# Cosine attention on one core: V cast two pairs at once, twelve sums of squares moved to TensorE, other ring sizes and new instruction orders

## The chip, the core and the metric

The kernel runs on one core of a Trainium2 chip. A core has five engines that work side by side: PE (TensorE, matmuls), ACT (ScalarE, functions such as the exponential), DVE (VectorE), POOL (GpSimd) and SP (SyncE, which here only issues DMAs). Each executes its own list of instructions strictly in order, and they wait for each other through semaphores. The metric is the device time of one execution in microseconds, lower is better. Before the change three runs took 189.35, 189.43 and 189.87 us: the median is 189.43 us.

## What is computed

```python
batch, heads, seq, dim = 8, 12, 512, 64          # float32 inputs, tau = 0.1
Q_norm = Q / (np.linalg.norm(Q, axis=-1, keepdims=True) + 1e-10)
K_norm = K / (np.linalg.norm(K, axis=-1, keepdims=True) + 1e-10)
scores = np.einsum('bhqd,bhkd->bhqk', Q_norm, K_norm) / tau
weights = np.exp(scores - np.max(scores, axis=-1, keepdims=True))
weights = weights / (np.sum(weights, axis=-1, keepdims=True) + 1e-10)
return np.einsum('bhqk,bhkd->bhqd', weights, V).astype(np.float32)
```

Scores of normalized vectors lie between -10 and 10, so the kernel takes no maximum off before the exponential.

## The kernel before

The 96 heads are worked on as 48 pairs of heads, numbered s = 0 to 47. For each pair:

- SP loads Q and K (256 KB each, `LD`, L311) and V (`LV`, L314), and stores the result (`ST`, L565).
- POOL squares Q and K of the pair in one instruction of 128x1024 (`SQ`, L337). The squares are summed over the 64 dimensions. For K this is done by PE in most pairs (`SSQ`, L354: eight small matmuls against the identity that fold 64 columns to 8, into columns 320 to 383 of one of the two accumulator banks of the values) followed by a small reduction on DVE (`RED`, L361). For Q from pair 4 on it is a reduction of 128x512 on DVE (`RED`, L365).
- For a group of one, two or four pairs DVE computes 1/norm by a few small instructions (`NEW`, L389 to L398).
- Q is scaled on DVE, K mostly on POOL (`SCL`, L420), into the ring `qn`. PE transposes both (`TR`, L426) into one PSUM bank, DVE copies that to SBUF (`EVA`, L434).
- The scores are made in four chunks of 128 keys (`SCO`, L508: two matmuls, one for each head, with 64 rows and 512 columns). Two chunks fit in PSUM. ACT takes the exponential of each chunk, 128x1024 (`EXP`, L531). A score chunk can start when the exponential of the chunk two before it is done.
- In pairs 37 and 45 chunk 3 is not done on ACT: its exponential is a polynomial on DVE and POOL (`SCX`, `X`, `Y`, L473 to L486).
- POOL casts V to bf16 (`VC`, L536) into `vb`, which carries a column of ones beside each block of 64 columns. PE multiplies the exponentials with it (`PV`, L548: eight groups of four matmuls, each group one block of 128 queries of one head, summed over the four chunks). Each head has its own accumulator bank.
- DVE takes the reciprocal of the sums (`RCP`, L559) and multiplies (`NRM`, L561) into the ring `ob`.

The next pair's values of the same head can start in a bank only after this pair's `NRM`, and, where an `SSQ` was placed in that bank behind the pair's values, after its `RED` too (`session`, `attached`, `bank_free`).

The program first lists all operations with what each needs. `ORDER` then gives, written out by hand as numbers, the order in which each engine executes them. Nothing is rescheduled at run time. The sizes of the rings stand in one line: `RINGS = 15, 10, 6, 4, 4, 4, 8, 3` for Q/K loads with cast V, V loads, squares, scaled Q and K, transposed Q and K, exponentials, output, and norms. An operation that fills a slot needs the last reader of what was in it, so for instance `LD` of pair s needs `SCL` and `SQ` of pair s - 15, and `NRM` of pair s needs `ST` of pair s - 8.

Of the kernel before, what the change touches and what calls it, by code (L numbers as in the profile page):

```python
# [5 lines left out]
ALU = mybir.AluOpType  # L6
# [13 lines left out]
class Program:  # L20
# [5 lines left out]
    def add(self, key, eng, kind, due, needs, emit, **kw):  # L26
        assert key not in self.ops, key
        op = Op(key, eng, kind, due, needs, emit, **kw)
        self.ops[key] = op
        self.list.append(op)  # L30
        return op

# [76 lines left out]
def bass_cosine_similarity_attention_kernel(  # L109
# [20 lines left out]
    qk = [sb(f"qk{i}", [128, 2, 2, NT * DIM], f32) for i in range(R_QK)]  # L130
    vf = [sb(f"vf{i}", [128, 2, NT * DIM], f32) for i in range(R_V)]
    vb = sb("vb", [128, R_QK, NT, 2, DIM + 1], bf16)
    sq = [sb(f"sq{i}", [128, 16, DIM], bf16) for i in range(R_SQ)]
    qn = [sb(f"qn{i}", [128, 2, NT, 2, DIM], bf16) for i in range(R_QN)]
# [16 lines left out]
    o_ps = [nc.alloc_psum_tensor(f"ops{b}", [128, 512], f32) for b in range(2)]  # L151
# [25 lines left out]
    def key(name, s, *rest):  # L177
# [9 lines left out]
        vb[:, :, :, :, DIM : DIM + 1].rearrange("p r c h o -> p (r c h o)"), 1.0))  # L187
# [14 lines left out]
    def due_red(s):  # L202
        return due_sq(s) + 2.0
# [9 lines left out]
    for s, w in sorted(((s, w) for s in range(NP) for w in range(2) if on_pe(s, w)), key=lambda j: (due_red(j[0]), j)):  # L213
        at = due_red(s) + 0.3
        if s < EARLY:
            early.append((s, w))
            continue
        due, i, h = next(x for x in slots if x[0] >= at and (x[1], x[2]) not in attached)
        attached[i, h] = (s, w)
        session[s, w] = (h, due, [("PV", i, h, NT - 1)])  # L220
# [5 lines left out]
    for s in range(NP):  # L226
        for h in range(2):
            bank_free[s, h] = before[h]
            before[h] = [("NRM", s, h)] + ([("RED",) + attached[s, h]] if (s, h) in attached else [])
# [67 lines left out]
    def pair(s):  # L297
# [6 lines left out]
        for w, x in ((0, Q), (1, K)):  # L304
            if s == 0:
# [8 lines left out]
              lambda e: e.dma_start(out=vf[iv][:, :, :], in_=src(V, s)), slot=f"v{iv}")  # L314
# [99 lines left out]
        for w in range(2):  # L414
# [3 lines left out]
            P.add(("SCL", s, w), "dve" if dve else "pool", "sclq" if dve else "sclk", T0 - (2.85 if w and not dve else 2.55) - slack(s, M_SCL),  # L418
                  [("NEW", g, (7 if direct_r(g) else 6) if acts and dve else 6 + w + (dve and w))] + ([("UNIT", s)] if s in off_of and w == 0 else []) + ([("TR", 0, w, 0), ("TR", 0, w, 1)] if s == R_QN else [key("TR", s - R_QN, w)]),
                  lambda e, w=w, r=r: e.tensor_tensor(  # L420
                      out=qn[iqn][:, w].rearrange("p t h d -> p h t d"),
                      in0=qk[iq][:, w].rearrange("p h (t d) -> p h t d", t=NT), in1=r, op=ALU.mult))
# [71 lines left out]
    def rest(s):  # L494
# [3 lines left out]
        for c in range(NT):  # L498
# [26 lines left out]
            for hs in ((0,), (1,)) if s == 0 and c < 2 else ((0, 1),):  # L525
# [9 lines left out]
        P.add(("VC", s), "pool", "vc", T0 + 3.0 - slack(s, M_VC), [("LV", s), key("PV", s - R_QK, 0, NT - 1), key("PV", s - R_QK, 1, NT - 1), "vone"],  # L535
              lambda e: e.tensor_scalar(  # L536
                  out=vb[:, iq, :, :, 0:DIM].rearrange("p c h d -> p h c d"),
                  in0=vf[iv][:, :, :].rearrange("p h (c d) -> p h c d", c=NT),
                  scalar1=1.0, scalar2=1.0, op0=ALU.mult, op1=ALU.mult))
# [3 lines left out]
        for h in range(2):  # L543
            for i in range(NT):
                def pv(e, h=h, i=i):
                    for c in range(NT):
                        t = i
                        last = e.matmul(  # L548
                            out=o_ps[h][:, 65 * t : 65 * t + 65],
                            lhsT=et[iet][:, c, h, 128 * t : 128 * t + 128], rhs=vb[:, iq, c, h, :],  # L550
                            start=(c == 0), stop=(c == NT - 1))
                    return last

                need, due = sum((exps(s, c) for c in range(NT)), []), T0 + PERIOD + 0.9 * PV_AT[4 * h + i] + late(s)
                P.add(("PV", s, h, i), "pe", "pv", due, need + [("VC", s)] + (bank_free[s, h] if i == 0 else [("PV", s, h, i - 1)]), pv)
            grid = o_ps[h][:, 0 : 65 * NT].rearrange("p (t x) -> p t x", x=65)
# [6 lines left out]
                      in1=rd[io][:, h, :].unsqueeze(2).to_broadcast([128, NT, DIM]), op=ALU.mult))  # L563
        P.add(("ST", s), "sp", "ld", s + STORE_AT, [("NRM", s, i) for i in range(2)],
              lambda e: e.dma_start(out=src(out, s), in_=ob[io][:, :].rearrange("p h t d -> p h (t d)")), slot=f"out{io}")  # L565

    def last(s, T0):
        iq, iet, io = s % R_QK, s % R_ET, s % R_O
        spare = t_ps[:, :, :, :].rearrange("p w t x -> p (w t x)").bitcast(f32)
        for k, (h, lo, hi) in enumerate(PIECES):  # L570
            bank = spare if k == 2 else o_ps[h]
            for c in range(NT):
                def pv(e, h=h, lo=lo, hi=hi, c=c, bank=bank):
                    for t in range(lo, hi):
# [3 lines left out]
                            rhs=vb[:, iq, c, h, :], start=(c == 0 and t == lo), stop=(c == NT - 1), skip_group_check=True)  # L578
# [29 lines left out]
OFF = {(45, 3): ((45, 45), False), (37, 3): ((37, 37), False)}  # L608
# [7 lines left out]
PE_BOTH = 4  # L616
BY_VECTOR = (35, 39, 43, 47)
Q_ON_PE = ()
# [3 lines left out]
RINGS = 15, 10, 6, 4, 4, 4, 8, 3  # L622
# [17 lines left out]
def slack(s, most):  # L640
# [5 lines left out]
        "7 8 64 65 103 104 11 141 142 66 179 180 105 222 223 143 256 257 181 298 299 224 332 333 258 375 376 300 "  # L646
        "409 410 334 451 452 63 377 102 411 140 453 178 221 485 486 527 528 561 562 487 604 605 529 638 639 255 "
        "563 680 681 297 606 714 715 331 640 756 757 374 682 790 791 408 716 833 834 450 758 867 868 484 792 901 "
        "902 526 835 935 936 560 869 978 979 603 903 1012 1013 637 937 1046 1047 679 980 1080 1081 713 1014 1122 "
        "1123 1048 1156 1157 1082 1190 1191 755 1124 1224 1225 789 1158 1267 1268 832 1192 1301 1302 866 1226 "  # L650
        "1335 1336 900 1269 1368 1369 934 1303 1411 1412 977 1337 1456 1457 1011 1370 1490 1491 1045 1413 1523 "
        "1524 1079 1458 1566 1567 1121 1492 1600 1601 1155 1525 1634 1635 1189 1568 1667 1668 1223 1602 1709 1710 "
        "1266 1636 1754 1755 1300 1669 1788 1789 1334 1711 1756 1790 1367 1410 1455 1489 1522 1565 1599 1633 1666 "
        "1708 1753 1787 1816 1830 "
    ),
    "pool": (
        "2 0 1 4 14 27 22 35 69 107 50 144 145 89 182 225 127 165 259 208 301 231 335 378 273 284 307 242 454 412 "
        "437 350 395 471 361 318 488 530 426 460 564 607 641 502 536 683 513 717 579 547 759 590 793 836 655 689 "
        "870 624 666 904 742 731 765 700 938 981 808 819 776 876 1015 1049 910 1083 853 887 921 1125 1066 953 "
        "1159 987 964 1021 1108 998 1193 1032 1304 1227 1338 1097 1270 1131 1165 1414 1371 1142 1199 1493 1242 "  # L660
        "1176 1310 1459 1569 1210 1343 1603 1253 1526 1287 1386 1321 1397 1354 1421 1637 1670 1465 1712 1436 1437 "
        "1438 1439 1476 1442 1509 1575 1552 1791 1586 1757 1609 1642 1740 1620 1684 1719 1653 1763 1774 1809 1695 "
        "1796 1734 1735 1736 1737 "
# [4 lines left out]
        "264 139 265 233 266 132 267 133 268 338 269 270 176 271 170 379 171 305 275 177 213 336 214 219 381 220 "  # L668
        "339 340 309 341 342 455 343 253 344 345 346 348 247 415 248 413 347 352 382 254 289 457 384 416 290 417 "
        "386 295 418 296 419 489 420 323 421 491 423 324 329 422 330 424 458 428 531 366 533 367 492 372 493 565 "  # L670
        "494 373 495 462 496 608 497 400 567 401 499 498 406 500 407 642 504 534 610 442 568 443 569 448 570 449 "
        "571 684 572 538 573 476 575 574 644 577 477 611 718 581 482 576 483 613 686 518 645 519 646 760 647 615 "
        "648 524 649 525 650 552 720 652 651 553 653 837 794 558 657 796 559 595 762 687 721 596 722 871 723 691 "
        "724 601 725 839 726 602 728 629 873 727 630 729 635 905 636 733 763 907 671 797 798 672 799 677 800 801 "
        "678 802 767 804 803 939 806 705 941 706 840 711 805 712 810 982 908 842 747 984 748 753 754 844 874 1050 "
        "781 1018 782 787 788 878 1016 1084 1052 824 942 825 943 944 912 945 830 946 831 947 949 948 950 951 858 "
        "1086 859 864 865 985 955 1019 1160 898 899 892 1128 893 1126 989 1055 1053 932 1162 933 926 927 1023 975 "
        "1194 976 1196 1087 969 1088 970 1089 1090 1305 1091 1057 1092 1228 1093 1094 1003 1095 1009 1004 1230 "
        "1010 1129 1339 1099 1340 1271 1043 1037 1273 1038 1044 1163 1133 1307 1197 1071 1231 1415 1232 1077 1072 "
        "1233 1078 1234 1372 1235 1167 1236 1119 1113 1238 1237 1120 1114 1240 1201 1308 1495 1274 1153 1239 1341 "  # L680
        "1374 1154 1147 1276 1148 1460 1244 1187 1494 1181 1417 1182 1570 1278 1462 1188 1375 1215 1376 1216 1377 "
        "1312 1378 1221 1379 1222 1380 1604 1382 1381 1345 1418 1384 1264 1419 1258 1265 1259 1383 1388 1463 1498 "
        "1527 1423 1292 1529 1298 1293 1431 1299 1432 1326 1572 1639 1434 1327 1435 1496 1638 1606 1713 1530 1332 "
# [86 lines left out]
```

## Time and profile before

| | us |
|---|---|
| median of three runs | 189.43 |
| the profiled execution | 189.84 |
| its span, first to last instruction | 187.9 |
| ACT busy | 180.8 |
| PE busy | 173.7 |
| DVE busy | 172.3 |
| POOL busy | 166.8 |

The page counts an engine as busy while it executes; waiting and issuing are not counted. Matmuls are pipelined, so PE's busy time is not its work. A group's row gives line, engine, operation, tiles out and in, shape and count, then busy time, the mean duration of one in ns, and the idle time before them with what ended it. The duration of one instruction can be longer than the distance from its start to the next one's start, as neighbours overlap. The chain that ended last is followed back from the last instruction; in order of time its rows are start, length and what ran. A timeline row is start, length, engine, line, operation and count.

Activity by stage (busy us and instructions of each engine, then granted clock, DMA share and GB/s), from the view of stretches:

```
15.00:60.00 45.00, 43.18 (x692) 27.31 (x688) 44.25 (x156) 45.00 (x52) 43.80 (x37) 1.00 1.04 344
60.00:96.00 36.00, 34.95 (x572) 22.58 (x568) 34.49 (x119) 36.00 (x41) 35.46 (x31) 1.00 0.96 311
96.00:140.00 44.00, 41.58 (x673) 26.48 (x673) 43.28 (x132) 44.00 (x49) 43.87 (x38) 1.00 0.96 320
140.00:176.00 36.00, 33.14 (x506) 20.14 (x505) 33.84 (x98) 35.99 (x40) 32.15 (x30) 1.00 0.38 121
176.00:187.90 11.90, 7.79 (x137) 5.04 (x136) 7.30 (x21) 8.46 (x11) 0.82 (x1) 1.00 0.34 112
```

The columns of engines are PE, PEld (weight loads), DVE, ACT and POOL.

### The profile page before, as it was taken

Reading aid. Unit: us, or ns where it says so; the run is one execution under the profiler, and the core shown is the slowest. Engines: PE = TensorE matmul, PEld = TensorE weight load, DVE = VectorE, ACT = ScalarE, POOL = GpSimd, SP = SyncE. Lnnn points to the kernel's source line nnn. Section 1 sums busy time; section 2 is a strip of 40 time slices with the busy share of each in tenths; the row PEclk is TensorE's granted clock in tenths of the full one; section 3 lists DMA queues with packets and bytes.
Section 4 is the critical chain, followed back from the end, with each engine's and each line's share of the span. In section 5 each row is a group of like instructions: output and inputs, shape, how many; then the busy total and the mean of one; then the engine's idle time right before and its main releaser. Section 6 shows DMA issues by size and latency. Waiting matters only on the chain.

```text
span 187.9 us, 6635 instructions
## 1 busy us (share of the span) xinstructions
PE 173.7 (92%) x2694; PEld 108.7 (58%) x2694; DVE 172.3 (92%) x546; ACT 180.8 (96%) x212; POOL 166.8 (89%) x152
## 2 busy tenths in 40 slices
PE   6999999999998999999999999899999989999983
PEld 2655666566665666666666556556645446655552
DVE  2789999999999999999999999999999999988864
ACT  4799999999999999999999999999999999999992
POOL 4797999999999999999999999999999999696600
PEclk9999999999999999999999999999999999999999
DMA  4999999899999988999999999976996551312215
GB/s 148 356 350 349 348 354 331 233 328 370 379 385 375 326 243 264 333 304 297 361 379 381 380 380 301 306 244 198 302 336 194 173 167 59 112 59 76 95 59 169
DMA packets 52446, 50.76 MB, mean 270 GB/s; under 512 B 3136, under 2 KB 52416, under 8 KB 52416
## 3 DMA queue, kind: packets, MB, share of 16 engines
q1 hardware_dynamic: 51984, 50.02, 81.1%
q8 instruction: 21, 0.34, 0.8%
q10 hardware_dynamic: 432, 0.33, 0.5%
q14 instruction: 9, 0.07, 0.1%
HBM read 37.75 MB, written 12.58 MB: 268 GB/s over the span
## 4 chain that ended last, share of the span: by engine, by line
ACT 92%; PE 4%; DMA 1%; DVE 1%; issue 1%; POOL 0%
ACT et L531 90%; DMA qk<-in_Q_dram 1%; PE ops L548 1%; PE scps L508 1%; DVE xs L245 0%; PE ops L576 0%; ACT ys L379 0%; DVE ob L589 0%; PE scps L268 0%; POOL qn L258 0%; ACT nps L382 0%; PE tps L268 0%; ACT sq L239 0%; ACT et L522 0%; PE scps L194 0%
## 5 line engine op out<-in xcount | busy, mean ns | idle before, releaser
L531 ACT ACTIVATE et<-scps 128x1024 bf16<-128x1024 f32 (+1 forms) x191 | 174.3, 1151 | 0.5 <-PE scps L508 0.5
L337 POOL TENSOR_TENSOR sq<-qk 128x1024 bf16<-128x1024 f32 x44 | 82.7, 1893 | 1.4 <-DMA qk<-in_K_dram 1.2
L508 PE MATMUL scps<-qt 64*128 64x512 bf16 x380 | 75.2, 386 | 7.8 <-ACT et L531 4.4
L548 PE MATMUL ops<-vb,et 128*128 128x65 bf16 x1504 | 71.6, 194 | 1.1 <-DVE qn L420 0.5
L548 PEld LDWEIGHTS ops<-vb,et 128*128 128x128 bf16 x1504 | 55.1, 98 | 27.1 <-issue 17.4
L420 POOL TENSOR_TENSOR qn<-qk,rk 128x512 bf16<-128x512 f32 x36 | 37.2, 1042 | 2.8 <-DVE rk L394 2.5
L561 DVE TENSOR_TENSOR ob<-ops,rd 128x256 f32<-128x256 f32 x94 | 38.9, 417 | 0.4
L420 DVE TENSOR_TENSOR qn<-qk,nps 128x512 bf16<-128x512 f32 x58 | 38.5, 677 | 0.4 <-ACT nps L382 0.4
L434 DVE COPY qt<-tps 128x1024 bf16<-128x1024 bf16 x47 | 32.3, 687 | 2.6 <-PE tps L426 2.1
L426 PE MATMUL tps<-ident,qn 128*128 128x128 bf16 x376 | 33.9, 221 | 0.1
L508 PEld LDWEIGHTS scps<-qt 64*128 64x128 bf16 x380 | 18.9, 92 | 26.0 <-ACT et L531 11.8
L365 DVE TENSOR_REDUCE nps<-sq 128x8 f32<-128x512 bf16 x48 | 32.3, 683 | 0.0
L536 POOL TENSOR_SCALAR vb<-vf 128x512 bf16<-128x512 f32 x48 | 30.8, 655 | 0.2
L426 PEld LDWEIGHTS tps<-ident,qn 128*128 128x128 bf16 x376 | 21.4, 98 | 12.9 <-issue 6.6
L559 DVE RECIPROCAL rd<-ops 128x4 f32<-128x4 f32 x94 | 16.2, 176 | 3.3 <-PE ops L548 2.3
L354 PE MATMUL ops<-sq,ident 128*128 128x64 bf16 x368 | 18.5, 194 | 0.0
L354 PEld LDWEIGHTS ops<-sq,ident 128*128 128x128 bf16 x368 | 13.9, 98 | 4.1 <-issue 2.7
L361 DVE TENSOR_REDUCE nps<-ops 128x8 f32<-128x64 f32 x40 | 8.5, 213 | 0.6 <-PE ops L354 0.5
L389 DVE TENSOR_TENSOR nps<-nps,ys 128x32 f32<-128x32 f32 (+1 forms) x30 | 6.3, 209 | 0.1
L390 DVE SCALAR_TENSOR_TENSOR nps<-nps,ys 128x32 f32<-128x32 f32 (+1 forms) x30 | 6.2, 208 | 0.1
L480 POOL TENSOR_TENSOR xz<-xz 128x1024 f32<-128x1024 f32 x2 | 3.8, 1892 | 1.5 <-DVE xz L475 1.5
L191 PE MATMUL ops<-warm_in,ident 128*128 128x512 bf16 x8 | 3.6, 628 | 1.4 <-POOL ident L181 1.4
(61 smaller groups left out, 65.0 us busy)
## 6 DMA issues: line engine op xcount, KB each, us to landing
vf<-in_V_dram SPq DMA_DIRECT2D x48, 256.0 KB, 5.8
qk<-in_Q_dram SPq DMA_DIRECT2D x47, 256.0 KB, 5.0
qk<-in_K_dram SPq DMA_DIRECT2D x47, 256.0 KB, 5.7
out_dram<-ob SPq DMA_DIRECT2D x47, 256.0 KB, 3.9
qk<-in_Q_dram SPq DMA_DIRECT2D x2, 128.0 KB, 2.7
qk<-in_K_dram ACTq DMA_DIRECT2D x2, 128.0 KB, 2.9
out_dram<-ob SPq DMA_DIRECT2D x1, 128.0 KB, 1.7
out_dram<-ob ACTq DMA_DIRECT2D x1, 64.0 KB, 1.6
```

The lines of the kernel that those rows point to most:

```text
L337: lambda e: e.tensor_tensor(out=sqf, in0=data, in1=data, op=ALU.mult))
L354: last = e.matmul(out=o_ps[bank][:, 320:384], lhsT=ident[:, :], rhs=sq[iqs][:, 8 * w : 8 * w + 8, 8 * k : 8 * k + 8], start=(k == 0), stop ...
L365: lambda e, w=w, dst=dst: e.tensor_reduce(out=dst, in_=sq[iqs][:, 8 * w : 8 * w + 8, :], axis=AX.X, op=ALU.add))
L420: lambda e, w=w, r=r: e.tensor_tensor(out=qn[iqn][:, w].rearrange("p t h d -> p h t d"), in0=qk[iq][:, w].rearrange("p h (t d) -> p h t d" ...
L426: last = e.transpose(t_ps[:, w, t, :], qn[iqn][:, w, t].rearrange("p h d -> p (h d)"), ident[:, :])
L434: lambda e: e.tensor_copy(out=qt[iqt][:, :, :, :].rearrange("p w t x -> p (w t x)"), in_=t_ps[:, :, :, :].rearrange("p w t x -> p (w t x)")))
L508: last = e.matmul(out=sc_ps[:, 2 * b + h, :], lhsT=qt[iqt][64 * h : 64 * h + 64, 1, c, :], rhs=qt[iqt][64 * h : 64 * h + 64, 0, :, :], sta ...
L531: lambda e, c=c, b=b, hs=hs: e.activation(out=et[iet][:, c, hs[0] : hs[-1] + 1, :], in_=sc_ps[:, 2 * b + hs[0] : 2 * b + hs[-1] + 1, :], f ...
L536: lambda e: e.tensor_scalar(out=vb[:, iq, :, :, 0:DIM].rearrange("p c h d -> p h c d"), in0=vf[iv][:, :, :].rearrange("p h (c d) -> p h c ...
L548: last = e.matmul(out=o_ps[h][:, 65 * t : 65 * t + 65], lhsT=et[iet][:, c, h, 128 * t : 128 * t + 128], rhs=vb[:, iq, c, h, :], start=(c = ...
L559: lambda e, h=h, grid=grid: e.reciprocal(out=rd[io][:, h, :], in_=grid[:, :, DIM]))
L561: lambda e, h=h, grid=grid: e.tensor_tensor(out=ob[io][:, h], in0=grid[:, :, 0:DIM], in1=rd[io][:, h, :].unsqueeze(2).to_broadcast([128, N ...
```

## The change

- Forty of the 48 casts of V, those of pairs 8 to 47, are done two pairs at a time by twenty instructions (`JOINT`). For this `vf` becomes one tensor, and `vb` is laid out by head before chunk. `join` makes one operation stand for both pairs: it needs both loads, and whoever needs one of the casts waits for the joint one.
- `Q_ON_PE` lists twelve pairs, 24 to 46 in steps of two, whose squares of Q are summed by `SSQ` on PE and a small `RED`, as those of K. The turns in the accumulator banks are given to K first and then to Q.
- The rings: Q/K loads and cast V 15 to 16, scaled Q and K 4 to 6, output 8 to 6.
- `BY_CHUNK`: in pairs 37 and 45 a group of value matmuls is one chunk for all four blocks of queries, with the polynomial chunk last, instead of one block of queries over all chunks. A group then needs only its own chunk's exponential.
- `ORDER` is new for PE, DVE, POOL and SP; ACT's is the same sequence of operations under new numbers. POOL's first change comes at the casts of pairs 10 and 11. SP's comes after the load of K of pair 40: the stores of pairs 27 to 30 follow the loads of pair 44, and those from 31 on follow the load of V of pair 47.
- Other new code does nothing in this version: joint scaling and joint normalization (`join2`, `"e"`) are listed for no pair, and `LATER` is empty.

```diff
+    def join(self, name, members, eng, kind, due, needs, emit, *rest):
+        op = self.add((name, members[-1]) + rest, eng, kind, due, needs, emit)
+        for s in members[:-1]:
+            self.ops[(name, s) + rest] = op
...
-    vf = [sb(f"vf{i}", [128, 2, NT * DIM], f32) for i in range(R_V)]
-    vb = sb("vb", [128, R_QK, NT, 2, DIM + 1], bf16)
+    vf = sb("vf", [128, R_V, 2, NT * DIM], f32)
+    vb = sb("vb", [128, R_QK, 2, NT, DIM + 1], bf16)
...
-    for s, w in sorted(((s, w) for s in range(NP) for w in range(2) if on_pe(s, w)), key=lambda j: (due_red(j[0]), j)):
+    for s, w in sorted(((s, w) for s in range(NP) for w in range(2) if on_pe(s, w)), key=lambda j: (j[0] >= EARLY and not j[1], due_red(j[0]), j)):
...
-        P.add(("VC", s), "pool", "vc", T0 + 3.0 - slack(s, M_VC), [("LV", s), key("PV", s - R_QK, 0, NT - 1), key("PV", s - R_QK, 1, NT - 1), "vone"],
-              lambda e: e.tensor_scalar(
-                  out=vb[:, iq, :, :, 0:DIM].rearrange("p c h d -> p h c d"),
-                  in0=vf[iv][:, :, :].rearrange("p h (c d) -> p h c d", c=NT),
-                  scalar1=1.0, scalar2=1.0, op0=ALU.mult, op1=ALU.mult))
+        both = [s - 1, s] if (s, "v") in JOINT else [s]
+        if (s + 1, "v") not in JOINT:
+            P.join("VC", both, "pool", "vc2" if len(both) > 1 else "vc", T0 + 3.0 - slack(s, M_VC),
+                   [("LV", i) for i in both] + [key("PV", i - R_QK, h, NT - 1) for i in both for h in range(2)] + ["vone"],
+                   lambda e: e.tensor_scalar(
+                       out=vb[:, iq + 1 - len(both) : iq + 1, :, :, 0:DIM].rearrange("p r h c d -> p (r h c) d"),
+                       in0=vf[:, iv + 1 - len(both) : iv + 1].rearrange("p r h (c d) -> p (r h c) d", c=NT),
+                       scalar1=1.0, scalar2=1.0, op0=ALU.mult, op1=ALU.mult))
...
                     for c in range(NT):
                         t = i
+                        if s in BY_CHUNK:
+                            t, c = c, last_chunk[i]
                         last = e.matmul(
                             out=o_ps[h][:, 65 * t : 65 * t + 65],
-                            lhsT=et[iet][:, c, h, 128 * t : 128 * t + 128], rhs=vb[:, iq, c, h, :],
-                            start=(c == 0), stop=(c == NT - 1))
+                            lhsT=et[iet][:, c, h, 128 * t : 128 * t + 128], rhs=vb[:, iq, h, c, :],
+                            start=(i == 0 and t == 0) if s in BY_CHUNK else c == 0,
+                            stop=(i == NT - 1) if s in BY_CHUNK else c == NT - 1, skip_group_check=s in BY_CHUNK)
...
-                need, due = sum((exps(s, c) for c in range(NT)), []), T0 + PERIOD + 0.9 * PV_AT[4 * h + i] + late(s)
+                last_chunk = [c for c in range(NT) if c != off_of.get(s)] + [off_of.get(s)]
+                need, due = exps(s, last_chunk[i]) if s in BY_CHUNK else sum((exps(s, c) for c in range(NT)), []), T0 + PERIOD + 0.9 * PV_AT[4 * h + i] + late(s)
...
+LATER = ()
+BY_CHUNK = (37, 45)
+JOINT = ((11, 'v'), (13, 'v'), (15, 'v'), (17, 'v'), (19, 'v'), (21, 'v'), (23, 'v'), (25, 'v'), (27, 'v'), (29, 'v'), (31, 'v'), (33, 'v'), (35, 'v'), (37, 'v'), (39, 'v'), (41, 'v'), (43, 'v'), (45, 'v'), (47, 'v'), (9, 'v'))
-Q_ON_PE = ()
+Q_ON_PE = (24, 26, 28, 30, 32, 34, 36, 38, 40, 42, 44, 46)
-RINGS = 15, 10, 6, 4, 4, 4, 8, 3
+RINGS = 16, 10, 6, 6, 4, 4, 6, 3
...
```

The end of PE's order, in names (pair, then chunk, or head and group; of the last pair piece and chunk), before:

```
SCO 46,2  PV 44,0,2  SCO 46,3  PV 44,0,3  SCO 47,0  PV 45,1,0-3  PV 45,0,0  SCO 47,1  PV 45,0,1-3  PV 46,1,0  SCO 47,2  PV 46,1,1-3  PV 46,0,0-3  SCO 47,3
```

and after:

```
SCO 46,2  PV 45,1,0-2  SCO 46,3  SCO 47,0  PV 45,1,3  PV 45,0,3  SCO 47,1  PV 46,1,0-3  SCO 47,2  PV 46,0,0-3  SCO 47,3
```

## The prediction

> **What bounds the kernel now.** I read the page's busy shares, its chain that ended last, the groups by cost, then the chain in order of time and the timeline where it leaves ACT.
>
> ```profile
> span 187.9 us, 6635 instructions
> ...
> PE 173.7 (92%) x2694; PEld 108.7 (58%) x2694; DVE 172.3 (92%) x546; ACT 180.8 (96%) x212; POOL 166.8 (89%) x152
> ...
> ACT 92%; PE 4%; DMA 1%; DVE 1%; issue 1%; POOL 0%
> ...
> L531 ACT ACTIVATE et<-scps 128x1024 bf16<-128x1024 f32 (+1 forms) x191 | 174.3, 1151 | 0.5 <-PE scps L508 0.5
> L337 POOL TENSOR_TENSOR sq<-qk 128x1024 bf16<-128x1024 f32 x44 | 82.7, 1893 | 1.4 <-DMA qk<-in_K_dram 1.2
> ```
>
> Four engines are near 90%, but the chain is ACT for 92% of the span: the exponentials (L531), one per score chunk, with 0.5 us idle before them in all.
>
> ```profile
> 15.22 149.65 ACT et L531 x163
> 164.86 0.01 issue
> 164.87 14.78 ACT et L531 x16
> 179.65 0.14 issue
> 179.79 0.39 PE scps L508 x2
> 180.18 0.72 PE ops L548 x20
> 180.90 0.32 PE scps L508 x2
> 181.22 0.59 PE ops L548 x16
> 181.81 0.32 PE scps L508 x2
> 182.13 0.96 PE ops L548 x28
> 183.09 0.34 PE scps L508 x2
> ```
>
> 149.65 us over 163 is 0.918 us each; where nothing delays them, neighbouring exponentials end 0.917 apart. The chain goes to PE only after 179.65: the values' matmuls of pair 45 (L548), held back by its chunk computed without ACT, crowd the last scores.
>
> So what can be won without fewer exponentials is what ACT loses. In the trace six of them after 15 us end later than 0.917 after their neighbour (chunk 1 of pairs 26, 30, 41; chunk 2 of 28, 42; chunk 0 of 42), by 0.03 + 0.03 + 0.10 + 0.06 + 0.12 + 0.04, in sum **0.36** with the roundings. At the end the last full one is over at 183.31 and the next begins at 183.45; neighbours normally overlap by 1.02 - 0.917 = 0.10, so **0.24** is lost there. How PE loses the race, before the longest of the six:
>
> ```profile
> 163.17 0.39 PE L508 MATMUL scps<-qt 64*128 64x512 bf16 x2
> ...
> 163.49 0.54 PE L548 MATMUL ops<-vb,et 128*128 128x65 bf16 x12
> ...
> 163.87 0.64 PE L426 MATMUL tps<-ident,qn 128*128 128x128 bf16 x8
> ...
> 164.44 0.39 PE L508 MATMUL scps<-qt 64*128 64x512 bf16 x2
> ```
>
> Start to start: a score pair holds PE for 0.32; twelve value matmuls 0.38, or 0.125 per four; eight transposes 0.57, being 0.23 per four and 0.10 of switch back to the score's shape. The interval is 1.27 where ACT's beat is 0.917. A group of eight square sums (L354) holds PE for 0.24 (97.26 to 97.50).
>
> **The change, part by part.** *V cast in twos.* Twenty POOL instructions replace forty. The group of single casts (L536) shows 0.655 us; a cast of 1,024 elements has no row. Its bounds are two singles, 1.31, and the nearest row, another one-input POOL operation on 1,024 elements:
>
> ```profile
> L479 POOL TENSOR_SCALAR xw<-xz 128x1024 f32<-128x1024 f32 x2 | 2.1, 1044 | 0.2
> ```
>
> I take 1.04: it is the same operation at that size. That frees 0 to 20 x 0.27 = 5.4 us of POOL. Worth on the path: 0. Only ACT and PE hold the chain after 15 us. The cover is the slack of casts and squares: adding up the new POOL order, the tightest joint casts (pairs 14 and 15, 20 and 21) are ready by 64.2 and 84.4, while the first value matmuls that read them start at 65.2 and 88.0 now. Were the cover of 1.0 gone, PE would stand for what a joint cast adds to the first of its two, 1.04 - 0.655 = 0.39. The first cast of each two also waits for the second V: the latest, V of pair 37, lands at 116.9 and is cast from about 120.
>
> *Squares of Q of twelve late pairs (24 to 46, even) on PE.* Each takes a reduction of 128x512 (L365, 0.683) off DVE and puts 0.213 (L361) there instead: 12 x 0.47 = 5.6 us less. PE gets 12 x 0.24 = 2.9 us more. DVE's saving is worth 0, for the reason above. PE's load matters: per pair four scores with switch (1.68), eight value groups (1.00), two transposes (0.46), one sum (0.24) make 3.38 of ACT's 3.67; a pair with two sums has 3.62. All twelve new sums go into bank 1 of the values' accumulators, and the next pair's values there wait for the reduction; between sum and that matmul stand two to four score chunks, 1.3 to 3.2 us.
>
> *Rings.* Scaled Q and K 4 to 6, Q/K loads 15 to 16: waits only fall away, worth 0 to a gain already inside the 0.60 below. The output ring falls from 8 to 6: the normalization of pair s needs the store of s - 6. Of the moved stores, those of 27 to 30 now stand behind the loads up to pair 44, and 31 onwards behind V of pair 47. SP then waits for pair 30's normalization (129.0 now) with V from 42 and Q/K from 45 queued behind it: after twelve more issues at 0.5 to 0.7 store 31 leaves by about 137, needed at 155.1. Q and K of 45 land by some 135; POOL would square them from about 135. That is the one tight spot; a us late there is covered by the 7 us until the sums are used. Cost 0.
>
> *Values of pairs 37 and 45 by chunk.* Same matmul count. Only the last of each eight groups waits for the chunk made off ACT, so six of pair 45's groups (6 x 0.125 = 0.75) leave the crowded end. Between the last scores the new order has 2, 4 and 4 value groups; 0.32 + 4 x 0.125 + 0.10 = 0.92 just keeps ACT's beat. I take the whole 0.24 back; bounds 0 and 0.24.
>
> *Orders anew.* ACT's order is the same. For PE I add, from one score to the next, the prices above and carry what exceeds 0.917. In the old order the carry reaches 0.40 (pair 28), 0.44 (41) and 0.47 (42), and ACT loses 0.06, 0.10 and 0.12 there: so a score may be about 0.34 late for nothing, and the rest is lost. In the new order the peaks are 0.45 and, after what is lost there, 0.42 (pairs 32, 33), 0.47 (41), and 0.35 to 0.36 three times (26, 40, 42): 0.11 + 0.08 + 0.11 + 0.05 = 0.35. Twice (before pairs 12 and 22) two value groups that need the very exponential the score needs stand ahead of that score; the two such places now (26, 30) lose 0.03 each: 0.06. Together **0.41**; bounds 0, and 0.8 if each is twice that.
>
> **Sum.** Against the profiled run's 189.84 (span 187.94 and 1.90 around it): -0.36 - 0.24 + 0.41 = -0.19, so 189.65. The median shown, 189.43, is 0.41 below that run; the forecast is **189.2**, with 188.8 to 189.7 as its own range.
>
> A rule of the Trainium skill reads PE otherwise: its page "Trainium Kernel Development and Optimization", section "Performance Expectations", says that matmul busy time misleads and that the share of weight loading is the better measure of PE. By that row PE is 58% taken, the twelve sums would cost nothing and 188.8 would result. The starts above, 3.38 of 3.67 us taken, speak against that reading here.
>
> **Rivals.** *Everything recovered* (188.8): no new stall, so -0.60 from 189.43 = 188.83. For it: freed POOL and DVE, deeper rings, and carries that barely pass 0.34. Against: none of the six losses of now needs POOL or DVE to explain it; PE's own work does; and PE gets more. This is also the floor, since the number of exponentials stays.
>
> *Bank 1 gated* (slower, 190.3). Place: the values of the pair after each new sum wait for its reduction, queued on DVE behind a transpose copy (L434, 0.687) or scaling. DVE must then do in 1.3 us: reciprocal 0.18, normalization 0.42, reduction 0.21 and one long operation 0.69, 1.5 in all: 0.2 late, which the 0.34 covers. A second long operation in that queue makes it 0.89, and ACT loses 0.55. The four tightest sums (26, 34, 38, 44) have only two score chunks of room; with two of them hit it is 189.2 + 1.1 = 190.3, with all 191.4. It decides from the second event on. For it: in front of the reductions of 38 and 44 stands just such a copy. Against: DVE has 5.6 us less to do, and those copies read transposes that PE does before the sum.
>
> *PE becomes the bound* (190.8). If a sum costs 0.33 (its start to a score's start) instead of 0.24, pairs with two sums need 3.80, 0.13 too much: 12 x 0.13 = 1.6, and 189.2 + 1.6 = 190.8. For it: PE's margin in pairs with two sums is 0.05. Against: every other pair has 0.29 free to catch up.
>
> That the joint cast costs two singles is within the forecast: it moves nothing on the path.
>
> **Chances.** Forecast 0.60, everything recovered 0.17, bank gated 0.15, PE bound 0.08. A measurement here tells about 0.3% (0.57 us) from no change: faster means below 188.86, slower above 190.0. Everything recovered ends just at the first bound and is counted there, as the forecast's lowest tenth would offset what falls short. Hence 0.17, 0.60, 0.23. Range 188.75 to 190.5: from just below the floor to most of the slower cases.
>
> **What would show it.** POOL: twenty casts of 16 x 64 near 1.04. DVE: 36 reductions of 128x512 instead of 48, 52 small ones instead of 40. ACT: exponentials still 0.917 apart, losses near pairs 32, 33 and 41, none at 28 and at the end. A chain with PE or DVE in it between 90 and 175 us for over 1 us would make the rivals right; a beat other than 0.917 or fewer exponentials would make the whole working wrong.

## The result and the profile after

Six runs of the changed kernel gave 190.72 to 191.21 us, median 190.86; six of the kernel before on the same chip 189.35 to 190.11, median 189.66. The ratio is 1.0065, with an interval of 1.0048 to 1.0082: 0.65% slower, where 189.2 us and no measurable change had been forecast. The time lies above the range of 188.75 to 190.5. The profiled run took 190.72 us (before: 189.84).

From the page of the changed kernel: the span, the engines' busy time, the shares of the chain that ended last, and the groups that answer to those shown before (busy us, mean ns of one, idle us ahead of them).

```profile
span 188.7 us, 6819 instructions
...
PE 176.4 (94%) x2790; PEld 112.6 (60%) x2790; DVE 170.6 (90%) x546; ACT 181.6 (96%) x212; POOL 163.6 (87%) x132
...
ACT 71%; DVE 12%; PE 10%; DMA 3%; issue 1%; SPq 1%
...
L555 ACT ACTIVATE et<-scps 128x1024 bf16<-128x1024 f32 (+1 forms) x191 | 175.3, 1067 | 0.2
...
L577 PE MATMUL ops<-vb,et 128*128 128x65 bf16 x1504 | 75.6, 195 | 1.1 <-DVE rd L592 0.3
...
L378 DVE TENSOR_REDUCE nps<-sq 128x8 f32<-128x512 bf16 x36 | 24.4, 679 | 0.0
L367 PE MATMUL ops<-sq,ident 128*128 128x64 bf16 x464 | 22.7, 193 | 0.0
...
L374 DVE TENSOR_REDUCE nps<-ops 128x8 f32<-128x64 f32 x52 | 11.2, 217 | 1.3 <-PE ops L367 1.0
```

Everything that was announced is there: 36 large reductions, 52 small ones, 96 more matmuls of squares. ACT's share of the chain fell from 92% to 71%. The one row that the prediction had not announced is L577: the same 1,504 value matmuls of the same shape are busy for 75.6 us, where they took 71.6 (L548 before).

The joint casts, from the groups with shapes kept apart:

```profile
L563 POOL TENSOR_SCALAR vb<-vf 128x1024 bf16<-128x1024 f32 x20 | 20.8, 1047 | 0.1
L563 POOL TENSOR_SCALAR vb<-vf 128x512 bf16<-128x512 f32 x8 | 4.9, 620 | 0.1
```

The chain of the changed kernel in order of time (start, length, what ran):

```profile
15.05 108.61 ACT et L555 x118
123.66 0.05 issue
123.71 0.39 PE scps L532 x2
124.10 0.33 PE tps L450 x4
124.43 0.63 PE ops L577 x16
125.06 0.32 PE scps L532 x2
...
127.86 0.62 PE ops L577 x16
128.48 0.23 PE ops L367 x8
128.71 0.32 PE scps L532 x2
129.03 0.36 PE ops L577 x8
129.40 0.45 PE tps L450 x8
129.84 0.34 PE scps L532 x2
```

Before, the chain stayed on ACT from 15.22 to 179.65, but for 0.01 us. Now it leaves ACT at 123.66 and runs over value matmuls, sums and transposes until 138 us. From 138.3 to 162.5 it lies on DVE for 20.1 us, and it comes back to ACT at 164.84:

```profile
161.32 0.41 DVE ob L594
161.74 0.14 DVE nps L403
161.87 0.60 DVE qt L458
162.48 0.05 issue
162.52 0.62 PE tps L450 x8
163.14 0.32 PE scps L532 x2
163.47 1.01 PE ops L577 x28
164.47 0.34 PE scps L532 x2
```

In that stretch DVE is busy for 23.90 of 24.20 us (23.59 before, where the chain stayed on ACT all the same). The transposes at 162.52 wait for DVE's copy of the pair before.

How much ACT lost can be read from the ends of neighbouring exponentials. Every end that comes 0.02 us or more later than 0.917 us after its neighbour's is a loss. In the kernel before they are 0.36 us in sum (counted alike for all kernels below), in the changed one **1.53 us**, over 21 places. The largest are, as pair and chunk: (32,3) 0.20, (42,1) 0.19, (41,0) 0.14, (33,2) and (41,1) 0.11 each, (22,0) 0.10, (12,3) 0.09, (27,0) 0.07.

A second measure serves for all runs: the **stretch** from the start of pair 2's first exponential to the end of the last full one. It leaves out the head, whose length varies from run to run (pair 2 began between 16.45 and 17.76 us in the profiles below), and the tail. It is 166.36 us before and 167.58 after; the changed kernel profiled a second time gave 167.58 again. So the loss is +1.22 us in the stretch and -0.25 in the tail (from the stretch's end to the span's: 4.63 before, 4.38 after), 0.97 together; the medians differ by 1.20, and by 1.05 where it was timed again.

### The profile page after: what moved, and what is told of

It is laid out like the page before. It is cut to its first block, busy times and chain, and to the rows that moved or that the text cites. A ratio compares the mean times of both kernels' runs of the same rounds, so it can differ in the third digit from the quotient of the medians.

```text
span 188.7 us, 6819 instructions
## 1 busy us (share of the span) xinstructions
PE 176.4 (94%) x2790; PEld 112.6 (60%) x2790; DVE 170.6 (90%) x546; ACT 181.6 (96%) x212; POOL 163.6 (87%) x132
## 4 chain that ended last, share of the span: by engine, by line
ACT 71%; DVE 12%; PE 10%; DMA 3%; issue 1%; SPq 1%
ACT et L555 71%; PE ops L577 4%; PE scps L532 3%; DMA qk<-in_Q_dram 3%; DVE ob L594 2%; DVE qn L444 2%; PE tps L450 2%; DVE qt L458 2%; DVE nps L378 1%; DVE et L510 1%; DVE nps L374 1%; PE ops L367 1%; DVE rd L592 1%; PE ops L618 1%; SPq L324 0%
## 5 line engine op out<-in xcount | busy, mean ns | idle before, releaser
L577 PE MATMUL ops<-vb,et 128*128 128x65 bf16 x1504 | 75.6, 195 | 1.1 <-DVE rd L592 0.3
L577 PEld LDWEIGHTS ops<-vb,et 128*128 128x128 bf16 x1504 | 57.5, 98 | 28.1 <-issue 18.3
L444 POOL TENSOR_TENSOR qn<-qk,rk 128x512 bf16<-128x512 f32 x36 | 38.1, 1070 | 5.4 <-DVE rk L407 5.2
L594 DVE TENSOR_TENSOR ob<-ops,rd 128x256 f32<-128x256 f32 x94 | 38.9, 417 | 1.0 <-DVE rd L592 0.3
L563 POOL TENSOR_SCALAR vb<-vf 128x1024 bf16<-128x1024 f32 (+1 forms) x28 | 25.7, 925 | 0.2
L378 DVE TENSOR_REDUCE nps<-sq 128x8 f32<-128x512 bf16 x36 | 24.4, 679 | 0.0
L367 PE MATMUL ops<-sq,ident 128*128 128x64 bf16 x464 | 22.7, 193 | 0.0
L367 PEld LDWEIGHTS ops<-sq,ident 128*128 128x128 bf16 x464 | 17.1, 98 | 5.5 <-issue 4.5
L374 DVE TENSOR_REDUCE nps<-ops 128x8 f32<-128x64 f32 x52 | 11.2, 217 | 1.3 <-PE ops L367 1.0
```

Of the source, the lines that this page charges most:

```text
L367: last = e.matmul(out=o_ps[bank][:, 320:384], lhsT=ident[:, :], rhs=sq[iqs][:, 8 * w : 8 * w + 8, 8 * k : 8 * k + 8], start=(k == 0), stop ...
L378: lambda e, w=w, dst=dst: e.tensor_reduce(out=dst, in_=sq[iqs][:, 8 * w : 8 * w + 8, :], axis=AX.X, op=ALU.add))
L444: lambda e, w=w, r=r: e.tensor_tensor(out=qn[iqn][:, w].rearrange("p t h d -> p h t d"), in0=qk[iq][:, w].rearrange("p h (t d) -> p h t d" ...
L563: lambda e: e.tensor_scalar(out=vb[:, iq + 1 - len(both) : iq + 1, :, :, 0:DIM].rearrange("p r h c d -> p (r h c) d"), in0=vf[:, iv + 1 - ...
L577: last = e.matmul(out=o_ps[h][:, 65 * t : 65 * t + 65], lhsT=et[iet][:, c, h, 128 * t : 128 * t + 128], rhs=vb[:, iq, h, c, :], start=(i = ...
L594: lambda e, h=h, grid=grid: e.tensor_tensor(out=ob[io][:, h], in0=grid[:, :, 0:DIM], in1=rd[io][:, h, :].unsqueeze(2).to_broadcast([128, N ...
```

## The experiments

Four theories: **T1**, the layout of `vb` by head makes value matmuls dearer, and PE has no room for it; **T2**, the twelve sums of Q fill PE; **T3**, the new orders themselves, through single overfull stretches or waits on DVE; **T4**, the joint cast.

"Spacing" is the median distance from the start of one group of four value matmuls to the next where one follows the other directly. All measurements first; the ratio is to the kernel before on the same chip:

| kernel | spacing, ns | ACT losses, us | stretch, us | ratio (interval) |
|---|---|---|---|---|
| before | 124 | 0.36 | 166.36 | 1 |
| changed | 129 | 1.53 | 167.58 | 1.0065 (1.0048 to 1.0082) |
| changed, again (e10) | 129 | 1.53 | 167.58 | 1.0051 (1.0034 to 1.0068) |
| e1 before, `vb` by head | 130 | 0.57 | 166.59 | 1.0010 (0.9997 to 1.0024) |
| e2 changed, single casts, by chunk | 124 | 1.01 | 167.07 | 1.0025 (1.0011 to 1.0039) |
| e5 changed, single casts, by head | 129 | 1.63 | 167.63 | 1.0059 (1.0035 to 1.0082) |
| e6 changed, pitch 66 | 128 | 1.37 | 167.44 | 1.0035 (1.0017 to 1.0053) |
| e14 changed, pitch 68 | 125 | 1.09 | 167.13 | single run |
| e7, e11 changed, pitch 72 | 123 | 0.95, 0.91 | 166.97, 167.00 | 1.0023 (1.0004 to 1.0042) |
| e15 changed, pitch 80 | 123 | 0.91 | 167.00 | single run |
| e13 changed, chunks 0, 2, 1, 3 | 124 | 0.96 | 167.02 | single run |
| e3 changed, no sums of Q | 130 | 4.20 | 170.24 | 1.0196 (1.0171 to 1.0222) |
| e9 before, eleven sums of Q | 124 | 1.17 | 167.17 | 1.0065 (1.0044 to 1.0086) |
| e4 before, tail by chunk | 124 | 0.36 | 166.37 | 0.9984 (0.9973 to 0.9995) |
| e8 before, tail and moves on PE | 124 | 1.07 | 167.11 | 1.0012 (0.9991 to 1.0032) |
| e12 pitch 72, moves on PE | 123 | 1.09 | 167.13 | 1.0044 (1.0027 to 1.0061) |

### The layout alone, put in and taken out (e1, e2, e5)

e1 is the kernel before with this edit, and the other places that use `vb` altered to match:

```diff
-    vb = sb("vb", [128, R_QK, NT, 2, DIM + 1], bf16)
+    vb = sb("vb", [128, R_QK, 2, NT, DIM + 1], bf16)
...
-                            lhsT=et[iet][:, c, h, 128 * t : 128 * t + 128], rhs=vb[:, iq, c, h, :],
+                            lhsT=et[iet][:, c, h, 128 * t : 128 * t + 128], rhs=vb[:, iq, h, c, :],
```

> The kernel before with one edit: vb is laid out by head (pair, head, chunk, 65 columns) in place of by chunk (pair, chunk, head, 65); casts stay single, orders and sums stay. Theory T1 (the layout that the joint cast needs makes each value matmul dearer): the start-to-start spacing of two groups of four value matmuls goes from 124 to about 129 ns in the trace, and the time from 189.7 to 190.0 to 190.2 us, since this order has more room on PE than the new one (my carry sums by group price: +0.24 us at 129 ns). T2 (the twelve Q sums fill PE) and T3 (the new orders and their waits) and T4 (the joint cast itself): the spacing stays 124 ns and the time stays within 0.2 us of 189.7.

From the page of e1:

```profile
PE 174.1 (93%) x2694; PEld 110.0 (59%) x2694; DVE 172.2 (92%) x546; ACT 180.8 (96%) x212; POOL 166.6 (89%) x152
...
L548 PE MATMUL ops<-vb,et 128*128 128x65 bf16 x1504 | 73.7, 195 | 1.1 <-ACT et L531 0.5
```

The value matmuls are busy for 2.1 us more than the 71.6 before, and nothing but the layout was touched. The price of T1 is shown. In the old order it costs the stretch only 0.23 us, and the ratio, 1.0010, can't be told from 1; in the new order the same price costs more, as e2 shows.

e2 is the changed kernel with the layout by chunk put back and `JOINT = ()`:

> The changed kernel with its casts single again and vb by chunk as before; sums of Q, tail and orders as changed (each single cast stands where the joint one stood or at its own pair's place). T1: the spacing returns to 124 ns and about two thirds of the 1.2 us that the changed kernel lost against my forecast come back: 189.9 to 190.2 us. T2 and T3: PE stays as full or waits as before, 190.6 to 191.0 us. T4: like T1 in time, but with the spacing still at 129 ns.

```profile
L577 PE MATMUL ops<-vb,et 128*128 128x65 bf16 x1504 | 73.6, 194 | 1.2 <-DVE rd L592 0.3
...
L563 POOL TENSOR_SCALAR vb<-vf 128x512 bf16<-128x512 f32 x48 | 29.0, 625 | 0.2
```

(two groups of e2's page). The matmuls are back by 2.0 us, the spacing at 124 ns, and 0.51 us of the stretch are back: under half of the loss, less than the two thirds that T1 had claimed. The time came out in T1's range, 190.15 us, and under that of T2 and T3. The other 2.0 us over the 71.6 of before stay, and aren't a price per group: the values stand in 161 separate stretches in place of 152, and each stretch's last matmul counts with its whole length, 0.19 us where a step is 0.03, which by estimate makes 9 x 0.16 = 1.4 us. Since this edit undoes the joint cast too, e5 undoes only that (`JOINT = ()`, layout by head):

> The changed kernel with single casts in place of the joint ones, vb still by head: the joint cast alone is undone. T1 (the layout costs, the joint cast as such does nothing): the spacing of the value matmuls stays at 129 ns and the time stays with the changed kernel, ratio to before 1.005 to 1.008. T4 (the joint cast is late for somebody): the time falls to the ratio of the run with single casts and the old layout, 1.0025.

Spacing 129 ns and a stretch of 167.63 against 167.58: the joint cast as such costs nothing on the path, and T4 falls. (With single casts, e2 and e5 alike, 0.07 to 0.08 us is lost at (7,3).)

### Which property of the layout (e6, e7, e11, e13, e14, e15)

By chunk, the four blocks that a group reads lie 260 bytes apart; by head they touch, 130 bytes from start to start. The pitch can be widened with the joint cast kept:

```diff
-    vb = sb("vb", [128, R_QK, 2, NT, DIM + 1], bf16)
+    vb = sb("vb", [128, R_QK, 2, NT, 66], bf16)
...
-                            rhs=vb[:, iq, h, c, :],
+                            rhs=vb[:, iq, h, c, 0 : DIM + 1],
```

> The changed kernel with joint casts kept and each block of vb 66 columns apart in place of 65 (132 bytes in place of 130; 65 are still read). If the dearer value matmuls come from the odd block pitch (blocks that start at 2 bytes past a multiple of 4): spacing 124 ns and the ratio to before near 1.0025, as in the run with the old layout. If they come from something else in the order by head (neighbouring blocks of one head read one after another): spacing stays 129 ns and the ratio 1.0065.

> The same with blocks 72 columns apart (144 bytes, a multiple of 16). If the pitch of 66 brings 124 ns, this does too. If 66 stays at 129 and 72 gives 124, a wider alignment counts; if both stay at 129 to 130, the pitch within the four blocks is not what counts.

66 hardly helps (128 ns), 72 does (123 ns). So it isn't the odd pitch. Nor does alignment up to 128 bytes explain it: blocks 132 bytes apart start, counted from a group's first block, at the same remainders of 128 as blocks 260 bytes apart (each 4 further), and those are cheap. e13 leaves every byte where it is and changes only the order in which the four chunks are taken, of `vb` and with it of the exponentials that serve as weights:

```diff
-                    for c in range(NT):
+                    for c in (0, 2, 1, 3):
```

> The changed kernel with the four matmuls of each value group in the order of chunks 0, 2, 1, 3 in place of 0, 1, 2, 3; data, layout and pitch (65) unaltered. If reading two blocks that touch each other one after the other is what costs: the steps 0 to 2 and 1 to 3 are as in the kernel before, only 2 to 1 is between touching blocks, and the spacing of groups goes from 129 ns to 126 or less. If it is where the blocks lie, whatever the order: 129 ns stays.

> By head with blocks 68 columns apart (136 bytes; 6 bytes free between blocks; 65 and 66 gave 129 and 128 ns, 72 with 14 free bytes 123). If the free gap has to reach some 8 bytes or more: 127 to 129 ns. If a multiple of 8 bytes is enough: 123 to 124 ns.

> By head with blocks 80 columns apart (160 bytes, 30 free). If the gap between blocks is what counts: 123 to 124 ns as with 72, and the stretch from pair 2's first exponential to the last full one 167.0 us as there. If the pitch of 72 was luck: anything else.

The same seven groups of pair 40 on PE in the changed kernel's timeline (start, length, engine, line, operation, tiles, count):

```profile
163.08 0.39 PE L532 MATMUL scps<-qt 64*128 64x512 bf16 x2
163.40 1.07 PE L577 MATMUL ops<-vb,et 128*128 128x65 bf16 x28
164.40 0.39 PE L532 MATMUL scps<-qt 64*128 64x512 bf16 x2
```

and in e13's:

```profile
162.81 0.39 PE L532 MATMUL scps<-qt 64*128 64x512 bf16 x2
163.14 1.03 PE L577 MATMUL ops<-vb,et 128*128 128x65 bf16 x28
164.10 0.39 PE L532 MATMUL scps<-qt 64*128 64x512 bf16 x2
```

Start of the values to start of the next score: 1.00 us and 0.96. With the order of reading alone the spacing is 124 ns, the stretch 167.02, the ACT losses 0.96. The page of e13 has the value matmuls at

```profile
L577 PE MATMUL ops<-vb,et 128*128 128x65 bf16 x1504 | 73.7, 195 | 1.2 <-DVE rd L592 0.3
```

where the changed kernel has 75.6. So the price needs both: blocks that touch, or nearly touch, and reading them in the order in which they lie. Where they lie doesn't make it alone (e13), nor does the order of the weights, which is the same in the kernel before and in the pitches. With 30 or 14 bytes free between blocks the price is gone, with 6 it is nearly gone (125 ns, between the two cases that e14 expected), with 2 it is there. Four ways of avoiding it (single casts by chunk, pitch 72, pitch 80, order of chunks) give back 0.51 to 0.61 us. e10 and e11 ran beside each other on one chip:

> The changed kernel once more, unaltered, beside the next run on the same chip: ratio 1.0065 within its interval, 190.9 us, spacing of value matmuls 129 ns, ACT losses 1.5 us.

> The changed kernel with the blocks of vb 72 columns apart, now timed. T1: the spacing is 123 ns, ACT losses 0.9 to 1.0 us as in the single look, and the ratio to before is 0.3 to 0.5% under that of the changed kernel beside it: 1.002 to 1.004. If the spacing doesn't decide, the two agree within 0.2%.

Their ratios, 1.0051 and 1.0023, differ as expected, but the intervals overlap; it is the stretch (167.58 and 167.00) that separates them.

### The sums of Q, taken out and put in (e3, e9)

```diff
-Q_ON_PE = (24, 26, 28, 30, 32, 34, 36, 38, 40, 42, 44, 46)
+Q_ON_PE = ()
```

> The changed kernel without the twelve Q sums on TensorE: 192 matmuls fewer (2.8 us of PE), and the DVE reductions of those pairs read all 512 columns again (each 0.46 us dearer on DVE). Joint casts, layout, tail and the rest of the orders stay. T2: most of the loss goes, 189.6 to 189.9 us. T1: the spacing stays at 129 ns; PE gets 2.8 us of room late in the run, so part of the loss goes, 190.0 to 190.5 us. T3: DVE is later, the waits on its norms grow, 190.8 us or more.

Slower by 2%, as only T3 had said (the edit takes out 96 matmuls; the expectation's 192 is wrong). The row of waits that grew most (from 25 to 176 us: who waited for whom, us in total, times, longest), first of the changed kernel, then of e3:

```profile
PEld ops L577 <- DVE ob L594: 2.9, 11, 0.5
```

```profile
PEld ops L577 <- DVE ob L594: 6.0, 17, 0.8
```

With the reductions back on DVE (12 x 0.46 = 5.6 us), the normalizations (L594) that free the accumulator banks come late, and the values wait for them. The new order leans on the relief of DVE. e3 therefore can't tell what the sums cost PE. e9 puts eleven of them into the kernel before (pair 46 finds no free turn there):

```diff
-Q_ON_PE = ()
+Q_ON_PE = (24, 26, 28, 30, 32, 34, 36, 38, 40, 42, 44)
...
-        due, i, h = next(x for x in slots if x[0] >= at and (x[1], x[2]) not in attached)
+        due, i, h = next(x for x in slots if (x[1:] == Q_SLOT[s] if not w else x[0] >= at and (x[1], x[2]) not in attached))
```

`Q_SLOT` gives each sum a turn in a bank behind a group of values; the orders are the old ones with the eleven sums set in.

> The kernel before with one part of the change alone: eleven of the twelve sums of Q (pairs 24 to 44, even, without 40's neighbour rules changed; pair 46 has no free bank slot in the old order) on TensorE, each behind a group of values of an earlier pair, its DVE reduction of 64 columns in place of 512 at the same bank's turn; nothing else is moved. PE gains 2.6 us of work, DVE loses 5.1 us. T2 (the sums fill PE): my carry sum gives +0.5 us over the stretches at pairs 24, 27, 28, 32, 41: ratio 1.002 to 1.004, ACT losses 0.9 us in place of 0.4. If DVE's relief is worth something in the old order: ratio under 0.998. If both are nothing there: 1.000.

The stretch grows by 0.81 us, ACT's losses from 0.36 to 1.17, more than the expectation gave T2 (its 1.002 to 1.004 against 1.0065). PE's waits for normalizations hardly change (the row shown for e3: 3.6 us in the kernel before, 3.7 in e9), so late accumulator banks don't explain it. What a second sum in one stretch does, on PE in the kernel before:

```profile
110.95 0.39 PE L508 MATMUL scps<-qt 64*128 64x512 bf16 x2
111.27 0.30 PE L548 MATMUL ops<-vb,et 128*128 128x65 bf16 x4
111.40 0.40 PE L354 MATMUL ops<-sq,ident 128*128 128x64 bf16 x8
111.73 0.39 PE L508 MATMUL scps<-qt 64*128 64x512 bf16 x2
```

and at the same place in e9:

```profile
111.05 0.39 PE L508 MATMUL scps<-qt 64*128 64x512 bf16 x2
111.37 0.30 PE L548 MATMUL ops<-vb,et 128*128 128x65 bf16 x4
111.51 0.63 PE L354 MATMUL ops<-sq,ident 128*128 128x64 bf16 x16
112.07 0.39 PE L508 MATMUL scps<-qt 64*128 64x512 bf16 x2
```

From score to score 0.78 us before and 1.02 with the second sum, over ACT's 0.917. And DVE's 4.0 us less work (172.3 to 168.3) buys nothing here. T2 holds as to the sums' cost in the old order. (The tail of e9's profile is 0.49 us longer too, 5.12 against 4.63. All of that lies between the end of the last normalization and the end of the span, 2.67 us against 2.18; why isn't known. The ratio contains it, so the stretch is the better measure of the sums.)

### The tail, and orders on PE (e4, e8, e12)

```diff
+                        if s in BY_CHUNK:
+                            t, c = c, last_chunk[i]
...
+BY_CHUNK = (45,)
```

> The kernel before with one part of the change alone: the value matmuls of pair 45 by chunk, with the closing instructions of PE and DVE ordered for that. My forecast's term for this part is -0.24 us: 189.4 us, with the stretch from the end of the last full exponential to the end of the span 0.2 us shorter than the 4.63 us before. If the tail's gain belongs to the new order and not to the values by chunk: 189.7 us.

Stretch 166.37, tail 4.38 against 4.63: -0.25 us, and a ratio of 0.9984. This part of the change does what it was forecast to do, and the kernel before with it alone is **the fastest version measured**, 189.41 us beside 189.79.

e8 moves seven operations on PE in e4's order (for instance both transposes of pair 44 to behind the last values of pair 40), e12 five groups of values in that of the changed kernel at pitch 72 (the two of pair 40 stand earlier by its edit, not later as its expectation says):

> The kernel before with the values of pair 45 by chunk (the run with the tail alone gave a ratio of 0.9984) and seven instructions of PE moved out of overfull stretches to the next roomy one, at pairs 26 to 28 and 41 to 43, where the kernel before loses its 0.4 us on ACT; old layout, single casts, no sums of Q. If PE overrun makes those losses: they fall to 0.1 us and the time is 0.6 us under before, ratio 0.997. If the losses come from waits on DVE: only the tail's gain, ratio 0.9984.

> As the run before, with five value groups of four matmuls moved on PE alone, each past one score chunk: of pair 31 to an earlier stretch, of pair 32 and 40 to a later one, and of pair 10 ahead of pair 11 (PE waited 0.4 us there for pair 11's exponentials). T3 in its PE form (the new order overfills single stretches): 0.2 us less than the run before, the losses at (12,3), (33,2), (42,1) gone. If the losses are due to DVE's waits: no change within 0.1 us.

Both missed. In e8 the old losses at pairs 26, 28 and 41 and at (42,2) are gone, but new ones arise, the largest 0.59 us at (43,0). Its timeline there:

```profile
166.18 0.69 DVE L434 COPY qt<-tps 128x1024 bf16<-128x1024 bf16 x1 [0.45 <-PE tps L426]
...
167.01 0.61 PE L426 MATMUL tps<-ident,qn 128*128 128x128 bf16 x8 [0.55 <-DVE rd L563]
...
168.25 1.02 ACT L531 ACTIVATE et<-scps 128x1024 bf16<-128x1024 f32 x1 [0.49 <-PE scps L508]
```

The delayed transposes of pair 44 kept DVE's copy waiting (0.45), that kept pair 45's transposes waiting (0.55), and so the score and ACT (0.49). In e12 the losses at (12,3), (33,2) and (42,1) are gone as expected, but 0.11 at (32,2) and 0.15 at (42,2) and (42,3) took their place, behind PE waits of 0.19 us for the normalization of pair 30 and of 0.32 for the scaling of pair 44. A sum over PE alone finds where it is overfull; where to put the work it doesn't tell.

## Why the prediction missed

Two steps failed. The new layout had no term in the sum; it cost 0.51 to 0.61 us. And the new orders with the sums in them, put at +0.05 us for the stretch, cost +0.61 to +0.71 us without the layout's price. Without it the kernel would have taken about 190.1 us (189.66 x 1.0023, from e11), still not faster. (Of the 1.66 us between 189.2 and 190.86, 0.23 is the base: the three runs on which the forecast rested had 189.43, all six 189.66.)

- **What bounds the kernel**: right as to ACT. Its beat stayed at 0.917 us, and the whole loss is exponentials that started late. But "only ACT and PE hold the chain after 15 us" doesn't carry over to the new order: between 123.66 and 164.84 us its chain lies on PE for 15.7 us and on DVE for 20.1. By the prediction's own sign (PE or DVE in the chain between 90 and 175 us for over 1 us) one of its rivals had come about.
- **The joint cast**: right. Taken at 1.04 us, measured 1.047; worth 0 on the path, measured +0.05 us of stretch when undone (e5).
- **The rings**: nothing speaks against the 0. From 25 to 176 us no engine that computes waits for a DMA in the changed kernel. No run changed the rings alone.
- **The new layout**: the first failed step. It was never priced: the change was costed as a POOL edit, and the value groups entered the new order at the 0.125 us that the old layout had shown. 376 groups at 5 to 6 ns more are about 2 us of PE (75.6 against 73.7 in e13, same orders), and in this order that costs 0.51 to 0.61 us.
- **Squares of Q on PE**: the unit price was right (0.24 forecast; 0.23 from one sum's start to the next sum, 0.24 to other work). DVE's saving at 0 was right for the old order (e9), but the new order needs that relief: without the sums it is 2.66 us longer (e3). The 2.9 us that PE gets were said to fit; eleven sums alone cost the old order 0.81 us.
- **Orders anew**: the second failed step. The term of +0.41 less 0.36 recovered was mis-sized, +0.05 for the stretch against +1.22. Taking the layout away leaves +0.61 to +0.71. The carry did name the places: at pairs 32 and 33 0.19 forecast and 0.22 measured in e13, at 12 and 22 0.06 and 0.10 (all of it at 12); at 41 0.11 against 0.20. (By its own rule the peak of 0.47 at 41 over 0.34 is 0.13, not 0.11; that changes little.) For pairs 26, 40 and 42 it had 0.05 together, where e13 lost 0.03 at (27,0), 0.12 at (40,2) and 0.15 at (42,1), and it had nothing for 0.08 at (43,0). In the stretches at 42 and 43 PE waited for DVE's copy of transposes or for a scaling (0.06 to 0.15 us each in e2). Such waits are not in a sum of prices. And the sum is steep: worked again for the values alone it gives about 0.33 us at 0.124 per group, 0.63 at 0.129 and 1.06 at 0.133, so it would have charged the layout some 0.30 us of the 0.51 to 0.61.
- **The six old losses** (-0.36): a third came back. Those of pairs 26, 28 and 30 (0.12 us) are gone; at 41 and 42 the new order loses 0.44 us in place of 0.26.
- **The tail** (-0.24): right, -0.25 in the changed kernel, -0.25 alone (e4).
- **The rivals**: "PE becomes the bound" named this outcome (190.8, chance 0.08) by another price: the sum did not cost 0.33, the values cost more. "Bank 1 gated" appears, PE waits of up to 0.3 us for normalizations at pairs 25, 28 and 30, but the losses behind them, at (27,0), (29,3) and (30,3), are 0.16 us of 1.53.
- The Trainium skill's page "Trainium Kernel Development and Optimization", section "Performance Expectations", names the share of weight loading, and beside it the share of the peak arithmetic, as measures of how close a kernel is to its limit. Taken as a measure of PE's room for more work, as the prediction's second reading took it, the share of weight loading fails in this kernel: it is 59% in e9 (58% before), and yet the sums alone cost 0.81 us. In-order starts, stretch by stretch, are what counted.

What stays open: how the remaining 0.6 to 0.7 us divides into the sums and the new order, as each is made for the other; how much of it is DVE's, which no run lightened in the new order between 138 and 162 us; and why reading touching blocks in turn costs TensorE time.

## What to carry to other kernels

When an edit on one engine forces a new layout, price every reader of that layout on the other engines; the rows of the old layout no longer hold. Where an in-order engine has a few per cent of room, total load decides little: add up its work from deadline to deadline, with its waits on other engines, and expect the result to swing: here by half a microsecond for 5 to 6 ns per group of four matmuls. Moving work off an engine that limits nothing gains nothing, but an order built around the lighter engine then can't do without it.

## What the runs showed that was not expected

Four value matmuls (65 columns of bf16 as the moving operand, accumulated into one block) that read touching blocks in turn take 129 to 130 ns from group to group; with the blocks read in the order 0, 2, 1, 3, or with 14 bytes free between them, 123 to 124. The steps tell where: from the third matmul to the fourth 33 and 32 ns (by head of the pair) in place of 29, and from the fourth to the next group's first 33 in place of 29; the first two steps, 29 to 30 and 34 to 36, are the same in both orders of reading. With 14 or 30 bytes free the median of the second step falls to 30 as well; with 6 bytes only the step to the next group stays dear (32 to 33). The dear steps are thus not simply those between touching blocks: the first two steps lead from a block to one that it touches and cost no more than before, and the step to the next group of the same head leads back to the first block, which the fourth doesn't touch. The runs show when the price is paid, not how it arises.
